# The values' projection: hi and lo weights side by side in one product of 512 columns, the halves added by GpSimd

## The chip, the core and the metric

The kernel runs on one core of a Trainium2 chip. The metric is the device time of one execution in microseconds. The core has TensorE (PE; its weight loads are shown as PEld), VectorE (DVE), ScalarE (ACT), GpSimd (POOL) and SyncE (SP). SP issues nearly all DMAs here; it, like every engine, works through its instructions in program order, and each waits on semaphores for what it reads or overwrites.

## The reference

A decoder block over 1024 tokens of width 1024, in float32. What matters here:

```
h = rms_norm(x, g_pre_mix)
z = h @ w_in
q, k, v, glu_in, z_ga, z_gc = split(z)
y_attn = dilated_attention_mixer(q, k, v, rel_bias_table, w_attn_out)
y_conv = conformer_conv_mixer(glu_in, ...)
merged = sigmoid(z_ga) * y_attn + sigmoid(z_gc) * y_conv
x = x + rms_norm(merged @ w_mix_out, g_post_mix)
x = x + rms_norm(swiglu_ffn(rms_norm(x, g_pre_ffn), w_ffn_in, w_ffn_out), g_post_ffn)
```

The values `v` are `h` (1024 x 1024) times 1536 columns of `w_in`: three dilated groups of eight heads of 64 columns.

## The kernel before

Every matrix product keeps float32 accuracy by splitting both operands in two parts, `hi` (rounded to fp32r) and `lo` (the rest), and adding three products: hi·hi, hi·lo and lo·hi. A split is a copy on ScalarE (hi) and a subtraction on VectorE or GpSimd (lo = x - hi).

Tiles of 128 x 1024 come from a pool of 42 slots (`slot()`, names `b`), of 3 (`ring()`, `d`) and, at half the width, of 11 (`half()`, `c`). Whoever takes a slot again waits for its last reader. PSUM has eight banks; in the stage at hand two of them have the tag `g` and serve the values' projection, two each `s`, `t` and `o` serve the attention.

The order on every engine is the order of the program text, written out by hand. `tick()` counts steps of work on TensorE: it runs what `later(n, step)` planned for that tick, takes one pending weight split from `pieces` at every fourth tick (`PIECE = 4`) and advances the background generators. `beat()` paces one generator more finely: every call adds `RATE` (0.42 in this stage) to a credit, and each whole credit advances `fine`, here `attention()`, by one step.

The program in order: the gate and GLU projections with the convolution beside them, the query and key projections (each stored to HBM), then the stage of the values, then the convolution's output projection, the attention's output projection, the mixing product, and the feed-forward part (its weight products are `unit`, L305 to L309, and `prod`, L321 to L323).

The stage of the values is six calls of `v(g, hg, now, then)`, one for each group and half of its heads. A call computes 8 tiles of 128 tokens by 256 columns, over KT = 8 slices of the contraction. Before the change, two tiles share a bank of 512 columns, in two accumulation groups; each slice is three products of 256 columns (L948: hi tokens with hi weights; L950: hi tokens with lo weights; L952: lo tokens with hi weights), each followed by a `beat()`, and every second slice by a `tick()`. After two tiles ScalarE copies the bank to a tile of the ring (L960 for group 0, L963 for the others); after four tiles, five ticks later, the tile goes to HBM (L933, L935). `timed()` loads the next call's weights at the fourth tick (L177) and queues their splits from the sixteenth tick on (`part()`, L188 and L189): each call has two weight tiles of 128 x 1024 (4 slices each), and each tile is split in two pieces of 512 columns.

Beside it run, in this order:

- `conv_norm()`, the normalisation of the convolution's output (L1265 to L1296): sums on TensorE, squares, `rstd()` (L402 to L411, transposes L417), then for each of eight blocks a product on VectorE (L1292), a SiLU on ScalarE (L1295) and a store (L1296).
- `attention()`, which starts in earnest when that is done (`normed` at 9). It goes over pairs of heads ("stacks"), eight query blocks each. `stack_load()` loads the queries' and keys' parts (L870 to L877) and the bias (L479); `double()` copies them to the other half of the partitions on GpSimd, two copies for each of two heads and each half of the tokens (L886, L887); `values()` loads the stored values (L898 to L903) and `value_parts()` splits them (ScalarE L917, GpSimd L918 and L922). The first stack is doubled directly before its first scores; a later one during query blocks 6 and 7 of the stack before.
- Per query block: scores on TensorE (`att_s`, L1049), bias and minimum on VectorE (L1052), one step later the exponential on ScalarE (`att_e`, L1062), four steps later transposes on TensorE (`att_t`, L1087) and a split (L1094, L1095), five steps later the products with the values (`att_p`, L1122).

`wsplit`, the engine that takes the subtraction of second weight pieces, is GpSimd while the queries and keys are projected and VectorE in the stage of the values.

Of the kernel before, what the change touches and what calls it, by code (L numbers as in the profile page):

```python
# [58 lines left out]
def f(ap):  # L59
    return ap.bitcast(F32)  # L60


class Build:
# [115 lines left out]

    def part(self, i, c):  # L180
        nc = self.nc
        n = self.jobs[i][1]
        s = slice(c * n // 2, (c + 1) * n // 2)
        if c == 0:
            self.hl[i] = (self.slot(F32R), self.slot(F32R))
        hi, lo = self.hl[i]
        r = self.raw[i]
        nc.scalar.copy(hi[:, s], r[:, s])  # L188
        (nc.vector if c == 0 else self.wsplit).tensor_tensor(lo[:, s], r[:, s], f(hi[:, s]), op=OP.subtract)  # L189
        if c == 1:  # L190
            del self.raw[i]

# [732 lines left out]
    def v(self, g, hg, now, then):  # L925

        nc = self.nc
        W = self.timed(now, then, 4, 16)

        def out(i, x):  # L930
            for e in range(2):
                if g == 0:
                    nc.sync.dma_start(self.d_v[g, 2 * hg + e][:, (i - 2) * 128:(i + 2) * 128], x[:, e * H:(e + 1) * H])  # L933
                    continue
                nc.sync.dma_start(self.d_v[g, 2 * hg + e].rearrange("(t p) c -> p t c", p=128)[:, i - 2:i + 2],  # L935
                                  x.rearrange("p (t e c) -> p t e c", t=4, e=2)[:, :, e])
            self.vn += i == 6

        for i in range(0, 8, 2):
            ps = self.bank()  # L940
            for e in range(2):
                t = slice((i + e) * 128, (i + e + 1) * 128)
                o = ps[:, e * 256:(e + 1) * 256]
                for kt in range(KT):
                    hi, lo = W[kt // 4]
                    s = slice((kt % 4) * 256, (kt % 4 + 1) * 256)
                    a, b = self.hH[kt][:, t], self.hL[kt][:, t]
                    nc.tensor.matmul(o, a, hi[:, s], start=kt == 0, stop=False)  # L948
                    self.beat()
                    nc.tensor.matmul(o, a, lo[:, s], start=False, stop=False)  # L950
                    self.beat()
                    nc.tensor.matmul(o, b, hi[:, s], start=False, stop=kt == KT - 1)  # L952
                    self.beat()
                    if kt % 2:
                        self.tick()
            if i % 4 == 0:
                x = self.ring()

            if g == 0:
                nc.scalar.copy(x.rearrange("p (e t c) -> p t e c", e=2, t=4)[:, i % 4:i % 4 + 2],  # L960
                               ps.rearrange("p (t e c) -> p t e c", t=2, e=2))
            else:
                nc.scalar.copy(x[:, (i % 4) * 256:(i % 4) * 256 + H], ps)  # L963
            if i % 4:
                self.later(5, lambda i=i, x=x: out(i, x))
                x = None

# [433 lines left out]
def build(ctx, tc, aps):  # L1401
# [18 lines left out]
    ga = [pair(NGA + n, NGA + n + 1) for n in range(0, 8, 2)]  # L1420
    gc = [pair(NGC + n, NGC + n + 1) for n in range(0, 8 - LATE - EARLY, 2)]
    qkj = {(g, hp): pair(NK + 4 * g + hp, NQ + 4 * g + hp) for g in range(3) for hp in range(4)}
    vj = {(g, hg): (job(aps["w_v"][2 * g + hg, 0]), job(aps["w_v"][2 * g + hg, 1], kind="second"))
          for hg in range(2) for g in range(3)}
    late = [job(w_in[NGC + n]) for n in range(8 - LATE - EARLY, 8 - EARLY)]
    co = [job(aps["w_co"][n]) for n in range(8)]
# [107 lines left out]
    B.OT, B.merges = {}, []  # L1534
    cn = B.bg(B.conv_norm())
    att = B.attention()
    vs = list(vj.values()) + [late[:1] or co[:1]]
    for i, (g, hg) in enumerate(vj):
        B.v(g, hg, vs[i], vs[i + 1])
        if i == 0:  # L1540
            next(att)
            B.fine = att
        elif i == 4:
            assert cn not in B.gens
            cs = []
            B.later(16, lambda: cs.append(B.bg(B.conv_split())))
    B.RATE = RU

    B.PIECE = 3
# [485 lines left out]
```

## Time and profile before

| | us |
|---|---|
| median of 3 runs | 1713.83 (1711.94 to 1715.37) |
| the profiled execution | 1713.53 |
| its span in the profile | 1711.4 |
| stage of the values in it (first to last product of L948 to L952) | 550.8 to 793.8 |
| first scores of the attention | 615.1 |

How to read the rows shown below. In the page's first part an engine has its busy time, the share of the span and the number of instructions. A timeline row has start and duration in us, engine, line, operation, what is written and read (partitions x elements), the count, and in brackets the idle time before it with what ended it. A group's row ends in busy time and mean ns of one, and after the bar the idle time of the engine before its instructions. A row that begins with a stretch A:B has its length, then the busy time (and count) of PE, PEld, DVE, ACT and POOL, or of PE and PEld alone where only one line was asked for, then the granted TensorE clock, the busy share of the DMA engines and GB/s. A row of waits has who waited, for whom, total us, times, and the longest. In the chain of waits each row has start, duration and what the chain went through; "issue" is time for which the profile names no cause.

### The profile page before, as it was taken

To read this page: it belongs to the slowest core of one execution; us is meant where nothing else is said; L and a number is where in the kernel's file an instruction comes from. 1 tells how busy PE (TensorE), PEld (TensorE's weight loads), DVE (VectorE), ACT (ScalarE), POOL (GpSimd) and SP (SyncE) were. 2 spreads that over 40 slices of the span, in tenths; PEclk is the share of its full clock that TensorE was granted. 3 is DMA by queue.
4 is the path that set the end of the run, shared out by engine and by line. 5 is a ranking of instruction groups with operands and counts; after the bars stand their busy time and mean duration, and the time that the engine had idled before them with its cause. 6 is when DMAs were issued, how large, how long until landed. Compare 5 with 4: busy or idle time off the path is not lost.

```text
span 1711.4 us, 24544 instructions
## 1 busy us (share of the span) xinstructions
PE 1692.6 (99%) x8758; PEld 1437.4 (84%) x8758; DVE 1251.5 (73%) x2214; ACT 790.1 (46%) x1550; POOL 470.0 (27%) x373
## 2 busy tenths in 40 slices
PE   8999999999999999999999999999999999999998
PEld 6788888888888999999778888888888888888886
DVE  6789988888998667677885855775566556677686
ACT  6344344434444576676722436633333333354463
POOL 0017777887886124444300210000000000000000
PEclk9999999999999999999999999999999999999999
DMA  4352434455568887878998722123222322494334
GB/s 166 103 185 87 148 124 130 155 193 174 173 167 206 249 261 208 234 204 229 295 274 281 266 79 99 68 95 127 93 92 103 119 93 92 148 374 144 103 130 154
DMA packets 162422, 283.43 MB, mean 166 GB/s; under 512 B 47249, under 2 KB 78796, under 8 KB 162300
## 3 DMA queue, kind: packets, MB, share of 16 engines
q1 hardware_dynamic: 161644, 281.23, 51.9%
q8 instruction: 69, 1.13, 0.3%
q0 software_dynamic: 368, 0.37, 0.1%
q14 instruction: 53, 0.43, 0.1%
q10 hardware_dynamic: 288, 0.27, 0.0%
HBM read 191.10 MB, written 95.42 MB: 167 GB/s over the span
## 4 chain that ended last, share of the span: by engine, by line
PE 91%; DMA 3%; ACT 2%; DVE 2%; issue 1%; POOL 1%; SPq 0%; DVEq 0%; ACTq 0%; POOLq 0%
PE p L321 16%; PE p L322 16%; PE p L323 16%; PE p L1919 12%; PE p L1648 5%; PE p L305 4%; PE p L307 4%; PE p L309 4%; PE p L1122 3%; PE p L948 2%; PE p L950 2%; PE p L952 2%; PE p L1049 2%; PE p L1087 2%; DMA b<-xT 1%
## 5 line engine op out<-in xcount | busy, mean ns | idle before, releaser
L321 PE MATMUL p<-b,b 128*128 128x512 f32 x1204 | 468.6, 389 | 0.3 <-ACT c L340 0.3
L322 PE MATMUL p<-b,b 128*128 128x512 f32 x1204 | 468.4, 389 | 0.0
L323 PE MATMUL p<-b,b 128*128 128x512 f32 x1204 | 468.4, 389 | 0.0
L321 PEld LDWEIGHTS p<-b,b 128*128 128x128 f32 x1204 | 226.0, 188 | 47.9 <-ACT c L340 0.7
L323 PEld LDWEIGHTS p<-b,b 128*128 128x128 f32 x1204 | 226.0, 188 | 46.9
L322 PEld LDWEIGHTS p<-b,b 128*128 128x128 f32 x1204 | 226.0, 188 | 46.9
L1919 PE MATMUL p<-b,b 128*128 128x512 f32 x924 | 209.6, 389 | 0.0
L1919 PEld LDWEIGHTS p<-b,b 128*128 128x128 f32 x924 | 173.4, 188 | 36.0
L686 DVE SCALAR_TENSOR_TENSOR p<-b,par,p 128x511 f32<-128x511 f32 (+14 forms) x232 | 163.6, 739 | 0.0
L305 PE MATMUL p<-b,b 128*128 128x512 f32 x368 | 146.7, 399 | 1.4 <-ACT b L1242 1.2
L307 PE MATMUL p<-b,b 128*128 128x512 f32 x368 | 145.5, 395 | 0.0
L309 PE MATMUL p<-b,b 128*128 128x512 f32 x368 | 145.5, 395 | 0.0
L195 ACT CAST b<-d 128x1024 fp32r<-128x1024 f32 x86 | 90.4, 1051 | 105.1 <-POOL d L216 55.1
L196 POOL TENSOR_TENSOR b<-d,b 128x1024 fp32r<-128x1024 f32 x44 | 106.9, 2429 | 79.7 <-ACT b L195 72.4
L196 DVE TENSOR_TENSOR b<-d,b 128x1024 fp32r<-128x1024 f32 x42 | 51.3, 1222 | 101.0 <-ACT b L195 101.0
L948 PE MATMUL p<-b,b 128*128 128x256 f32 x384 | 112.8, 294 | 0.0
L952 PE MATMUL p<-b,b 128*128 128x256 f32 x384 | 112.2, 292 | 0.0
L950 PE MATMUL p<-b,b 128*128 128x256 f32 x384 | 112.2, 292 | 0.0
L1243 DVE TENSOR_TENSOR b<-b,b 128x512 fp32r<-128x512 f32 x133 | 91.6, 693 | 22.2 <-ACT b L1242 20.1
L1242 ACT CAST b<-b 128x512 fp32r<-128x512 f32 x133 | 82.1, 619 | 46.8 <-PE p L1919 18.0
L1648 PE MATMUL p<-b,b 128*128 128x512 f32 x384 | 89.4, 391 | 0.0
L1062 ACT ACTIVATE c<-c,stat 128x128 f32<-128x128 f32 (+1 forms) x192 | 85.0, 446 | 5.6 <-DVE stat L1052 5.3
(233 smaller groups left out, 2995.5 us busy)
## 6 DMA issues: line engine op xcount, KB each, us to landing
b<-w_in SPq DMA_DIRECT2D x30, 512.0 KB, 5.0
dk<-c SPq DMA_DIRECT2D x48, 256.0 KB, 2.9
dq<-c SPq DMA_DIRECT2D x48, 256.0 KB, 3.7
b<-dq SPq DMA_DIRECT2D x48, 256.0 KB, 5.1
b<-dk SPq DMA_DIRECT2D x48, 256.0 KB, 7.5
b<-w_fi SPq DMA_DIRECT2D x24, 512.0 KB, 5.0
d<-w_in SPq DMA_DIRECT2D x23, 512.0 KB, 4.3
dqS<-c SPq DMA_DIRECT2D x44, 256.0 KB, 2.0
```

The lines of the kernel that those rows point to most:

```text
L196: self.wsplit.tensor_tensor(lo, x, f(hi), op=OP.subtract)
L305: nc.tensor.matmul(ps, hi[:, s], a, start=kt == 0, stop=False)
L307: nc.tensor.matmul(ps, hi[:, s], b, start=False, stop=False)
L309: nc.tensor.matmul(ps, lo[:, s], a, start=False, stop=kt == nk - 1)
L321: nc.tensor.matmul(ps, hi[:, s], a, start=first and kt == 0, stop=False, skip_group_check=True)
L322: nc.tensor.matmul(ps, hi[:, s], b, start=False, stop=False, skip_group_check=True)
L323: nc.tensor.matmul(ps, lo[:, s], a, start=False, stop=kt == 3, skip_group_check=True)
L686: nc.vector.scalar_tensor_tensor(A[i][:, j:], src[i][:, :H - j], w[i], A[i][:, j:], op0=OP.mult, op1=OP.add)
L948: nc.tensor.matmul(o, a, hi[:, s], start=kt == 0, stop=False)
L950: nc.tensor.matmul(o, a, lo[:, s], start=False, stop=False)
L1648: nc.tensor.matmul(banks[tt][nh], st, wt[:, nh * H:(nh + 1) * H], start=bool(kt == 0 and a), stop=bool(kt == KT - 1 and b))
L1919: nc.tensor.matmul(acc[t], x, y, start=first and e == 0, stop=last and e == 2, skip_group_check=True)
```

## The change

The weights of the values are laid out in other order: for each slice of the contraction, 256 columns of hi and 256 of lo stand side by side. A slice is then two products: the hi tokens with all 512 columns into the whole bank (hi·hi in its left half, hi·lo in its right half), and the lo tokens with the 256 hi columns, accumulated on the right half. `beat()` is called three times per slice as before, twice after the first product and once after the second.

A bank now belongs to one tile of tokens. ScalarE copies it to one half of a new tile `vsum` (one slot, held for the whole stage); after every second tile GpSimd adds the left and right halves of both into the ring's tile. The stores wait for that add. The splits of these weights write to the new layout (`value_weights`), with the subtraction always on VectorE, and each weight tile is given up in the last token tile, slice pair by slice pair. `job(..., kind="values")` marks the first weight tile so that `part()` sends it there.

```diff
     def part(self, i, c):
         nc = self.nc
+        if self.jobs[i][2] in ("values", "second"):
+            return self.value_weights(i, c)
...
+    def value_weights(self, i, c):
+
+        x = self.slot(F32R)
+        self.hl.setdefault(i, []).append(x)
+        r = self.raw[i][:, c * H:(c + 1) * H].rearrange("p (k n) -> p k n", k=2)
+        d = x.rearrange("p (k e n) -> p k e n", k=2, e=2)
+        self.nc.scalar.copy(d[:, :, 0], r)
+        self.nc.vector.tensor_tensor(d[:, :, 1], r, f(d[:, :, 0]), op=OP.subtract)
+        if c == 1:
+            del self.raw[i]
...
     def v(self, g, hg, now, then):
...
-        W = self.timed(now, then, 4, 16)
+        W = [x for w in self.timed(now, then, 4, 16) for x in w]
...
-        for i in range(0, 8, 2):
-            ps = self.bank()
-            for e in range(2):
-                t = slice((i + e) * 128, (i + e + 1) * 128)
-                o = ps[:, e * 256:(e + 1) * 256]
-                for kt in range(KT):
-                    hi, lo = W[kt // 4]
-                    s = slice((kt % 4) * 256, (kt % 4 + 1) * 256)
-                    a, b = self.hH[kt][:, t], self.hL[kt][:, t]
-                    nc.tensor.matmul(o, a, hi[:, s], start=kt == 0, stop=False)
-                    self.beat()
-                    nc.tensor.matmul(o, a, lo[:, s], start=False, stop=False)
-                    self.beat()
-                    nc.tensor.matmul(o, b, hi[:, s], start=False, stop=kt == KT - 1)
-                    self.beat()
-                    if kt % 2:
-                        self.tick()
-            if i % 4 == 0:
+        for i in range(8):
+
+            ps = self.bank()
+            t = slice(i * 128, (i + 1) * 128)
+            for kt in range(KT):
+                w = W[kt // 2][:, kt % 2 * H:(kt % 2 + 1) * H]
+                a, b = self.hH[kt][:, t], self.hL[kt][:, t]
+                nc.tensor.matmul(ps, a, w, start=kt == 0, stop=kt == KT - 1, skip_group_check=True)
+                self.beat()
+                self.beat()
+                nc.tensor.matmul(ps[:, 256:], b, w[:, :256], start=False, stop=kt == KT - 1, skip_group_check=True)
+                self.beat()
+                w = None
+                if kt % 2:
+                    if i == 7:
+                        W[kt // 2] = None
+                    self.tick()
+            nc.scalar.copy(self.vsum[:, i % 2 * H:(i % 2 + 1) * H], ps)
+            if i % 2 == 0:
+                continue
+            if i % 4 == 1:
                 x = self.ring()
 
+            y = self.vsum.rearrange("p (t k n) -> p k t n", t=2, k=2)
+            d = x[:, i % 4 // 2 * H:(i % 4 // 2 + 1) * H].rearrange("p (t n) -> p t n", t=2)
             if g == 0:
-                nc.scalar.copy(x.rearrange("p (e t c) -> p t e c", e=2, t=4)[:, i % 4:i % 4 + 2],
-                               ps.rearrange("p (t e c) -> p t e c", t=2, e=2))
-            else:
-                nc.scalar.copy(x[:, (i % 4) * 256:(i % 4) * 256 + H], ps)
-            if i % 4:
+                y = y.rearrange("p k t (e c) -> p k e t c", e=2)
+                d = x.rearrange("p (e t c) -> p e t c", e=2, t=4)[:, :, i % 4 - 1:i % 4 + 1]
+            nc.gpsimd.tensor_tensor(d, y[:, 0], y[:, 1], op=OP.add)
+            if i % 4 == 3:
                 self.later(5, lambda i=i, x=x: out(i, x))
                 x = None
...
     att = B.attention()
+
+    B.vsum = B.slot()
     vs = list(vj.values()) + [late[:1] or co[:1]]
...
+    B.vsum = None
     B.RATE = RU
```

The stores' slices and the count `vn` are shifted by one tile accordingly, from `i - 2 : i + 2` at i = 6 to `i - 3 : i + 1` at i = 7.

More of the change, by code (lines that the diff above doesn't have):

```diff
@@ L932, in out @@
                 if g == 0:
-                    nc.sync.dma_start(self.d_v[g, 2 * hg + e][:, (i - 2) * 128:(i + 2) * 128], x[:, e * H:(e + 1) * H])
+                    nc.sync.dma_start(self.d_v[g, 2 * hg + e][:, (i - 3) * 128:(i + 1) * 128], x[:, e * H:(e + 1) * H])
                     continue
-                nc.sync.dma_start(self.d_v[g, 2 * hg + e].rearrange("(t p) c -> p t c", p=128)[:, i - 2:i + 2],
+                nc.sync.dma_start(self.d_v[g, 2 * hg + e].rearrange("(t p) c -> p t c", p=128)[:, i - 3:i + 1],
@@ L936, in out @@
                                   x.rearrange("p (t e c) -> p t e c", t=4, e=2)[:, :, e])
[L937 to L939 removed]
+            self.vn += i == 7
+        for i in range(8):
             ps = self.bank()
[L941 to L956 removed]
+            t = slice(i * 128, (i + 1) * 128)
[16 more added lines that the diff above has]
+            if i % 4 == 1:
@@ L1422, in build @@
     qkj = {(g, hp): pair(NK + 4 * g + hp, NQ + 4 * g + hp) for g in range(3) for hp in range(4)}
-    vj = {(g, hg): (job(aps["w_v"][2 * g + hg, 0]), job(aps["w_v"][2 * g + hg, 1], kind="second"))
+    vj = {(g, hg): (job(aps["w_v"][2 * g + hg, 0], kind="values"), job(aps["w_v"][2 * g + hg, 1], kind="second"))
           for hg in range(2) for g in range(3)}
```

## The prediction

> **What bounds the kernel now.** I read the page first, then the stage that the diff touches, then what every other engine and queue does around it. The page:
>
> ```profile
> span 1711.4 us, 24544 instructions
> PE 1692.6 (99%) x8758; PEld 1437.4 (84%) x8758; DVE 1251.5 (73%) x2214; ACT 790.1 (46%) x1550; POOL 470.0 (27%) x373
> PEclk9999999999999999999999999999999999999999
> ```
>
> TensorE sets the end nearly everywhere, at full granted clock. The profiled execution took 1713.53 us, 2.1 us more than its span; the median shown is 1713.83 (1711.94 to 1715.37), so the two agree and I add my sum to 1713.53.
>
> The stage of the values is found by its first product (L948), once for each of 6 calls x 8 token tiles x 8 slices of the contraction = 384:
>
> ```profile
> 550.70:612.70 62.00, 45.83 (x160) 30.65 (x161) 1.00 0.87 264
> 612.70:794.10 181.40, 66.96 (x224) 42.43 (x224) 1.00 0.78 222
> ```
>
> 160 = 2 x 64 + 32, so at 612.70 two calls and half of the third are done, almost alone on TensorE: 62 us for 160 slices. The other 224 slices take 181 us, because from 615 on the attention's products stand between them. What the other engines do meanwhile, in the order PE, PEld, DVE, ACT, POOL:
>
> ```profile
> 552.00:590.00 38.00, 38.00 (x310) 37.04 (x309) 23.87 (x27) 17.14 (x25) 7.74 (x8) 1.00 0.93 282
> 600.00:614.00 14.00, 14.00 (x119) 14.00 (x118) 5.41 (x6) 7.57 (x9) 0.00 (x0) 1.00 1.01 309
> 630.00:670.00 40.00, 40.00 (x371) 40.00 (x371) 28.71 (x91) 26.25 (x82) 18.04 (x26) 1.00 0.74 207
> ```
>
> In the mixed part ScalarE is busy two thirds, VectorE 72%, GpSimd 45%: room for more work, if it isn't late. Before 615 GpSimd is all but idle and the DMA engines are full (1.01). Both matter below. The row of the order in which TensorE meets the attention:
>
> ```profile
> 601.07 0.28 PE L952 MATMUL p<-b,b 128*128 128x256 f32 x1
> ...
> 612.71 0.28 PE L948 MATMUL p<-b,b 128*128 128x256 f32 x1
> ...
> 614.99 0.28 PE L950 MATMUL p<-b,b 128*128 128x256 f32 x1
> 615.11 0.56 PE L1049 MATMUL p<-b,b 128*128 128x128 f32 x4
> 615.50 0.33 PE L952 MATMUL p<-b,b 128*128 128x256 f32 x1
> ...
> 620.39 0.74 PE L1049 MATMUL p<-b,b 128*128 128x256 f32 x4 [0.63 <-DVE stat L1052]
> ...
> 622.45 0.83 PE L1122 MATMUL p<-c,b 128*66 128x256 f32 x3 [0.40 <-POOL b L918]
> ```
>
> The displayed 0.28 us of a product is latency. What it costs TensorE is the distance of starts: 612.71 to 614.99 is 19 distances, 0.120 us each. The attention's first products (L1049) come at 615.11, after 20 products of the fifth tile (i = 4) of the third call. The only idle TensorE time in the stage is the 0.63 and 0.40 us while the attention's pipeline fills.
>
> **The change, part by part.** *The products.* For the price of 512 columns with a fresh stationary operand, the feed-forward part:
>
> ```profile
> 1299.83 0.39 PE L322 MATMUL p<-b,b 128*128 128x512 f32 x1
> ...
> 1303.91 0.39 PE L322 MATMUL p<-b,b 128*128 128x512 f32 x1
> ```
>
> This is 18 distances in 4.08 us, 0.2267 us each. A slice costs 3 x 0.1200 = 0.3600 now and 0.2267 + 0.1200 = 0.3467 then: 13.3 ns saved. The columns streamed stay 768; what goes is one product's fixed share. Over 384 slices: -5.1 us. The displayed means (294 for 256 columns, 389 for 512) would promise 384 x 0.2 = 76 us; they are latencies, and I don't use them. The attention's steps are paced by three calls of beat() per slice as before, so their number and the weight loads exposed after them stay.
> The Trainium skill, "TensorE: Matmul & The Clock Gate", section "Back-to-back issue gap", gives a warm product N/2.4 + 2.5 ns. By it three products of 256 cost 327 and the pair 325 ns, and the gain would be 0.9 us, the sum 4.2 us higher; the measured distances of 120 and 227 have about 13 ns of fixed share, so I keep 5.1.
>
> *Copies, adds and splits.* Prices from the stage's groups:
>
> ```profile
> L963 ACT COPY d<-p 128x512 f32<-128x512 f32 x15 | 8.7, 583 | 6.5 <-PE p L952 6.3
> L960 ACT COPY d<-p 128x512 f32<-128x512 f32 x8 | 4.7, 588 | 7.8 <-PE p L952 7.7
> L918 POOL TENSOR_TENSOR b<-b,b 128x512 fp32r<-128x512 f32 x18 | 23.1, 1282 | 100.2 <-ACT b L917 85.1 <-PE p L1122 7.9 <-ACT c L1062 7.2
> L189 DVE TENSOR_TENSOR b<-b,b 128x512 fp32r<-128x512 f32 x22 | 15.6, 711 | 15.1 <-ACT b L188 14.6 <-POOL b L886 0.2
> ```
>
> ScalarE empties a bank per tile: 48 copies for 24, 24 x 0.585 = 14 us more in 243. GpSimd gets 24 adds of 1.28 us, 31 us. The weight splits keep count and size; the second half of the first jobs moves from GpSimd to VectorE, where one takes 0.71 us; 0, and 0.71 us if the first slices wait for it. None of this is on TensorE's path by its sum. Its order is.
>
> *What the add is put in front of.* GpSimd now, over the whole early stage, and ScalarE around 614:
>
> ```profile
> 549.19 2.39 POOL L708 TENSOR_TENSOR b<-b,b 128x1024 f32<-128x1024 f32 x1
> 574.03 1.43 POOL L886 CAST b<-b 64x512 fp32r<-64x512 f32 x1 [22.46 <-DMA b<-dq]
> ...
> 583.07 0.61 POOL L887 CAST b<-b 64x512 fp32r<-64x512 f32 x1
> 619.58 1.28 POOL L918 TENSOR_TENSOR b<-b,b 128x512 fp32r<-128x512 f32 x1 [35.89 <-ACT b L917]
> ...
> 622.75 0.61 POOL L886 CAST b<-b 64x512 fp32r<-64x512 f32 x1
> ...
> 627.79 0.61 POOL L887 CAST b<-b 64x512 fp32r<-64x512 f32 x1
> ```
>
> ```profile
> 593.04 1.08 ACT L1288 COPY b<-p 128x512 f32<-128x512 f32 x2 [2.93 <-PE p L417]
> ...
> 603.88 0.56 ACT L963 COPY d<-p 128x512 f32<-128x512 f32 x1
> ...
> 607.75 0.56 ACT L963 COPY d<-p 128x512 f32<-128x512 f32 x1
> 614.13 0.62 ACT L188 CAST b<-b 128x512 fp32r<-128x512 f32 x1 [5.82 <-issue]
> 614.65 0.58 ACT L963 COPY d<-p 128x512 f32<-128x512 f32 x1
> 615.25 1.28 ACT L1062 ACT_TABLE_LOAD   x1
> ```
>
> ```profile
> 606.91 1.42 DMA b<-w_v
> 608.32 5.81 issue
> ```
>
> The eight copies of double() (L886, L887) for the first pair of heads run at 574 to 584, over 30 us before TensorE needs them, because GpSimd has nothing ahead of them but L708. In the program they stand directly before the first L1049, in tile 4 of the third call. The change queues ten adds ahead of them; the last (i = 3 of that call) waits for ScalarE's copy of tile 3, and that copy stands behind L188, the first split of the next call's weights, issued at the sixteenth tick (the end of tile 3). L188 waits until 614.13; the chain has a load of w_v before it, and the DMA engines are full, so I read it as that load's landing.
>
> So: L188 at 614.13, copy at 614.65 to 615.23, add of 1.28 us to 616.5, then copies at a distance of 0.72 us: (627.79 - 622.75) / 7. Both heads' first halves need four, 2.9 us: 619.4. Then L1049's last two products, 0.2 us: TensorE is past its first step at 619.6, where it is at 615.50 now: +4.1. The 167 slices before that point had saved 2.2 us; that is swallowed by the wait, as are bank waits earlier on. (Two banks now hold one tile each, 2.8 us of work. Today's lag from 601.07 to the copy at 603.88 and its 0.56 us, 3.4 us, would then hold TensorE about 0.6 us, and is paid in full if the wait at 613 isn't there.) Bounds for the landing: it comes 1.3 us earlier, as TensorE reaches the transposes (L417) that ScalarE's chain starts from after some 96 faster slices, or not at all. I take -0.4, since full queues keep their own pace. Then 217 slices more: -2.9.
>
> Two further terms. The 1.03 us of idle time in the filling pipeline goes or stays: the table load has time before the first scores now, but one more copy of 0.58 is in ScalarE's queue; between -1.0 and +0.6, I take 0. In the mixed part 14 more copies and 13 adds stand in the queues before the attention's work; if each held TensorE for a copy's 0.585 us that is 8.2, if none 0. Nearest is 0, since ScalarE has a third of its time free and GpSimd half, and a tile lasts 181 / 28 = 6.5 us: only an add behind a whole run of eight doubles (0.6 + 5.7 + 1.3 us after the tile) comes late for the next even tile, by 1.1 us; I take +0.7.
>
> The slot for vsum takes one of 42 from the loads. SP does wait for slots:
>
> ```profile
> SPq L870 <- PE p L952: 6.7, 1, 6.7
> ```
>
> That load is the first heads' stacks, needed 30 us later; one more such wait costs nothing here, and up to 6.7 us where a load is late already. The output stores wait for the add instead of the copy, 1.3 us, and stand five ticks behind: 0.
>
> Sum: +4.1 - 0.4 - 2.9 + 0 + 0.7 = +1.5, so 1715.0 us. The likeliest outcome is that the gain pays for the late start of the attention.
>
> TensorE would then stand idle for some 4 us, up from 1.
>
> ```profile
> 0.00:5.00 5.00, 0.00 (x0) 0.00 (x0) 0.54 (x4) 1.86 (x3) 2.17 (x12) 1.00 0.58 173
> ```
>
> The granted clock is 1.00 in every stretch, and also in these 5 us without a product, so no row shows a loss after an idle time. The Trainium skill, same page, section "What's actually happening", has the clock go to half after an idle window of 3.4 us and return after as much work: by it about 1.7 us more, 1716.7.
>
> **The rivals.** *Faster: the wait isn't there.* If the load lands 4 us earlier, the copy of tile 3 starts at 610.9 with the tile's end, the add ends at 612.8, four copies at 615.7, TensorE goes on at 615.9, +0.4, and with -2.9 and the +0.7 the end is 1711.7. If GpSimd's copies are out of the way altogether, all 5.1 us arrive: 1708.4. For it: the unnamed 5.81 us may be another thing than the load. Against it: the order on GpSimd, which is fixed by the program.
>
> *Slower: the eight copies at their price of 574.* There the first took 1.43 us, not 0.61, with the DMA engines as full as at 614. Four at 1.5 us instead of 0.72 are 3.1 us more: 1718.1. It decides from about 1.3 us each. Against it: at 622.75 they take 0.61.
>
> *Slower: ScalarE and GpSimd late in the mixed part.* The single vsum makes the copy of an even tile wait for the add before, and everything on ScalarE behind it: the upper bound of 8.2 instead of 0.7 gives 1722.5, half of it 1718.4. For it: GpSimd works in runs of eight copies, 5.7 us, and the attention's exponentials and casts share ScalarE's queue. Against: a tile's 6.5 us.
>
> *No gain from the wide product.* Then +2.9 is not given back: 1717.9 or more. The measured 0.2267 us speaks against it. And behind the stage the DMA engines are full:
>
> ```profile
> 834.00:844.00 10.00, 8.73 (x64) 7.12 (x63) 9.47 (x37) 6.63 (x24) 1.39 (x2) 1.00 1.04 397
> ```
>
> TensorE misses 1.3 us there now, so a shift of a few us may be stretched or absorbed by about as much; this widens every case.
>
> **How the numbers follow.** Late start paid by the gain: 0.45, with 1711.5 to 1718 as its own range. Faster: 0.22 (1708.4 to 1711.7). Copies at the dear price: 0.15. Late queues in the mixed part: 0.14. No gain: 0.04. Within 0.2% (3.4 us, what a measurement of this kernel can tell from no change) of 1713.83 is 1710.4 to 1717.3. The main case lies there but for 0.05 at its top; the faster case reaches over with 0.04; of the slower ones 0.03 falls short of it. Faster 0.18, same 0.47, slower 0.35. The range from 1708.5 to 1721 leaves the ends of the outer cases out.
>
> **What would show it.** Right: the first L886 after 615 and after an add; an idle TensorE of 3 to 5 us before the first L1049, ended by GpSimd; distances of 0.227 and 0.120 in the values' products; 48 copies and 24 adds near 0.58 and 1.28 us. Wrong: the doubles still at 574, no idle time there, or a new idle time at a bank in every tile.

## The result, and the profile after

| | us, median | beside before | ratio, 95% interval |
|---|---|---|---|
| changed kernel, first measurement, 16 runs | 1718.79 (1715.03 to 1722.06) | 1713.78 | 1.0033 [1.0024, 1.0041] |
| changed kernel, second measurement, 11 runs | 1716.35 (1714.41 to 1718.21) | 1713.21 | 1.0019 [1.0010, 1.0027] |

The change makes the kernel slower, by 0.2 to 0.3%: 5.0 us by the first measurement's medians, 3.1 by the second's. The forecast was 1715.0 with a range from 1708.5 to 1721; both medians lie in the range, above the forecast, and the first also lies above 1718, where the prediction's likeliest case ended; by the bound of 0.2% the first is slower and the second at its edge. The profiled execution took 1717.66 us, its span 1715.9, 4.5 more than the span of before.

The first rows of the changed kernel's page:

```profile
span 1715.9 us, 23845 instructions
PE 1694.7 (99%) x8374; PEld 1414.1 (82%) x8374; DVE 1259.9 (73%) x2216; ACT 802.2 (47%) x1574; POOL 496.4 (29%) x395
```

TensorE has 384 instructions fewer and is busy 2.1 us longer. The number of products alone therefore says little of the time; the place to look is where TensorE stands. Stretches of the stage in the changed kernel (length, then PE, PEld, DVE, ACT, POOL, granted clock, DMA share, GB/s):

```profile
600.00:614.00 14.00, 12.55 (x71) 10.46 (x70) 8.00 (x7) 10.14 (x12) 2.89 (x2) 1.00 0.94 276
616.00:619.30 3.30, 1.20 (x6) 0.68 (x4) 0.69 (x1) 2.04 (x3) 2.34 (x3) 1.00 1.09 385
619.30:626.10 6.80, 6.20 (x23) 5.54 (x24) 3.11 (x16) 3.56 (x12) 3.81 (x7) 0.51 1.06 345
630.00:670.00 40.00, 40.00 (x327) 36.25 (x326) 29.38 (x90) 28.75 (x87) 20.66 (x27) 1.00 0.65 178
```

There are two holes, one in 600 to 614 (before: full) and one in 616 to 619.3, and behind the second the granted clock is 0.51 for 6.8 us. In 630 to 670 TensorE is full again, though ScalarE and GpSimd have more to do than before. The same in the changed kernel's timeline of TensorE (L959 is the product of 512 columns, L962 the one of 256; in brackets the idle time and what ended it):

```profile
548.40 0.39 PE L336 MATMUL p<-b,b 128*128 128x512 f32 x1
548.98 0.50 PE L334 MATMUL p<-b,b 128*128 128x512 f32 x1 [0.19 <-DVE c L853]
...
560.59 0.40 PE L959 MATMUL p<-b,b 128*128 128x512 f32 x1
560.83 0.28 PE L962 MATMUL p<-b,b 128*128 128x256 f32 x1
...
562.71 0.40 PE L959 MATMUL p<-b,b 128*128 128x512 f32 x1
...
601.14 0.28 PE L962 MATMUL p<-b,b 128*128 128x256 f32 x1
602.84 0.50 PE L959 MATMUL p<-b,b 128*128 128x512 f32 x1 [1.42 <-ACT b L969]
...
616.48 0.39 PE L959 MATMUL p<-b,b 128*128 128x512 f32 x1
618.84 0.33 PE L1066 MATMUL p<-b,b 128*128 128x128 f32 x1 [1.97 <-POOL b L899]
619.51 0.47 PE L1066 MATMUL p<-b,b 128*128 128x128 f32 x1 [0.34 <-POOL b L900]
620.17 0.48 PE L1066 MATMUL p<-b,b 128*128 128x128 f32 x1 [0.20 <-POOL b L899]
620.84 0.47 PE L1066 MATMUL p<-b,b 128*128 128x128 f32 x1 [0.19 <-POOL b L900]
621.12 0.52 PE L962 MATMUL p<-b,b 128*128 128x256 f32 x1
```

A slice is one of each: six slices from 560.59 to 562.71 are 0.353 us each, 0.236 and 0.117. The scores (now L1066) start at 618.84, and each of their four products waits for one of GpSimd's copies; TensorE is past this step at 621.12, where before it was at 615.50. Of the two queues that set this, the changed kernel's timeline of ScalarE:

```profile
615.65 0.62 ACT L201 CAST b<-b 128x512 fp32r<-128x512 f32 x1 [3.18 <-DMA b<-w_v]
616.18 0.58 ACT L969 COPY b<-p 128x512 f32<-128x512 f32 x1
```

And its timeline of GpSimd:

```profile
616.84 1.28 POOL L980 TENSOR_TENSOR d<-b 128x512 f32<-128x512 f32 x1 [4.99 <-ACT b L969]
618.18 0.60 POOL L899 CAST b<-b 64x512 fp32r<-64x512 f32 x1
618.84 0.61 POOL L900 CAST b<-b 64x512 fp32r<-64x512 f32 x1
```

Read in order of time, this is the chain of the prediction link by link: the load of w_v lands and releases the split (L201) at 615.65, the bank's copy follows at 616.18, the add at 616.84, and the first of the eight doubles (L899), at 574.03 before, only at 618.18. The groups of the copies and adds between 550 and 800 us have about the prices that were used (the adds before 600 take up to 1.78 us, hence the mean of 1379 ns):

```profile
L980 POOL TENSOR_TENSOR d<-b 128x512 f32<-128x512 f32 x23 | 31.7, 1379 | 79.7 <-ACT b L969 60.2 <-DMA b<-dq 6.6 <-PE p L1139 6.4
L969 ACT COPY b<-p 128x512 f32<-128x512 f32 x48 | 28.0, 583 | 18.3 <-PE p L962 16.6 <-POOL d L980 1.5
```

For comparing kernels I use five points of TensorE's timeline, in us: the first product of the values (A), the first product of the values after the attention's first scores (B), the second pair's first scores (C), the last product that begins a slice of the values (D) and the end of the span (E).

| | A | B | C | D | E | A to B | B to C | C to D | D to E |
|---|---|---|---|---|---|---|---|---|---|
| before | 550.77 | 615.50 | 629.37 | 793.29 | 1711.4 | 64.73 | 13.87 | 163.92 | 918.1 |
| changed | 551.83 | 621.12 | 635.93 | 799.09 | 1715.9 | 69.29 | 14.81 | 163.16 | 916.8 |
| changed, second profile | 551.51 | 620.38 | 634.43 | 797.60 | 1714.8 | 68.87 | 14.05 | 163.17 | 917.2 |

The loss is in A to B, +4.6 and +4.1 us. C to D gives back 0.8. A itself lies between 550.7 and 552.3 in the profiles of all the kernels below, so that its 1.1 is mostly spread between executions.

### The profile page after: what moved, and what is told of

Same layout as the page of the kernel before. It is cut to its first block, busy times and chain, and to the rows that moved or that the text cites. A ratio compares the mean times of both kernels' runs of the same rounds, so it can differ in the third digit from the quotient of the medians.

```text
span 1715.9 us, 23845 instructions
## 1 busy us (share of the span) xinstructions
PE 1694.7 (99%) x8374; PEld 1414.1 (82%) x8374; DVE 1259.9 (73%) x2216; ACT 802.2 (47%) x1574; POOL 496.4 (29%) x395
## 4 chain that ended last, share of the span: by engine, by line
PE 93%; DMA 2%; DVE 2%; ACT 1%; issue 1%; POOL 1%; SPq 0%; DVEq 0%; ACTq 0%; POOLq 0%
PE p L334 15%; PE p L335 15%; PE p L336 15%; PE p L1939 12%; PE p L1668 5%; PE p L318 5%; PE p L320 5%; PE p L322 5%; PE p L959 5%; PE p L1139 3%; PE p L962 2%; PE p L1066 2%; PE p L569 2%; PE p L1104 2%; DMA dact<-b 1%
## 5 line engine op out<-in xcount | busy, mean ns | idle before, releaser
L334 PE MATMUL p<-b,b 128*128 128x512 f32 x1204 | 468.8, 389 | 0.5 <-ACT c L353 0.3
L335 PE MATMUL p<-b,b 128*128 128x512 f32 x1204 | 468.4, 389 | 0.0
L336 PE MATMUL p<-b,b 128*128 128x512 f32 x1204 | 468.4, 389 | 0.0
L1939 PE MATMUL p<-b,b 128*128 128x512 f32 x924 | 209.6, 389 | 0.0
L959 PE MATMUL p<-b,b 128*128 128x512 f32 x384 | 150.2, 410 | 1.4 <-ACT b L969 1.4
L318 PE MATMUL p<-b,b 128*128 128x512 f32 x368 | 146.6, 398 | 1.3 <-ACT b L1259 1.2
L320 PE MATMUL p<-b,b 128*128 128x512 f32 x368 | 145.6, 396 | 0.0
L322 PE MATMUL p<-b,b 128*128 128x512 f32 x368 | 145.5, 395 | 0.0
L962 PE MATMUL p<-b,b 128*128 128x256 f32 x384 | 116.0, 302 | 0.0
L1668 PE MATMUL p<-b,b 128*128 128x512 f32 x384 | 89.4, 391 | 0.0
L208 ACT CAST b<-b 128x1024 fp32r<-128x1024 f32 x47 | 49.5, 1052 | 82.0 <-POOL b L236 37.2
```

The source lines that it names most:

```text
L318: nc.tensor.matmul(ps, hi[:, s], a, start=kt == 0, stop=False)
L320: nc.tensor.matmul(ps, hi[:, s], b, start=False, stop=False)
L322: nc.tensor.matmul(ps, lo[:, s], a, start=False, stop=kt == nk - 1)
L334: nc.tensor.matmul(ps, hi[:, s], a, start=first and kt == 0, stop=False, skip_group_check=True)
L335: nc.tensor.matmul(ps, hi[:, s], b, start=False, stop=False, skip_group_check=True)
L336: nc.tensor.matmul(ps, lo[:, s], a, start=False, stop=kt == 3, skip_group_check=True)
```

## The experiments

The theory: the late start of the attention is the whole loss, and it comes from the order on GpSimd alone. The rivals: the longer way from the bank costs throughout the stage; the wide product is worth nothing; the clock's drop is the loss. Each diff is against the changed kernel unless it says otherwise.

**The doubles ahead of the adds.** The add stays on GpSimd; the eight copies are put into its queue as soon as the convolution's normalisation has begun.

```diff
+        doubled = False
...
                     while self.normed < 9 or x is None:
+                        if not doubled and self.normed:
+                            doubled = True
+                            self.double(nxt, 0)
+                            self.double(nxt, 1)
...
-                    if cur is None:
-                        self.double(nxt, 0)
-                        self.double(nxt, 1)
```

> The first stack's eight copies of double() are put on GpSimd as soon as the first block of the normalisation is done, some 15 us before the first scores; all else as in the changed kernel. Theory (the loss is the order on GpSimd, plus the half clock that follows the idle time): no wait before the first scores, which come at about 616.7 instead of 618.84, TensorE past the first step at 617.1 instead of 621.1, granted clock 1.00 throughout; time 4 to 6 us under the changed kernel, about 1713 to 1715, no different from before. Rival (the loss is in banks, copies and the mixed part): time stays above 1717.

Measured: 1714.04, ratio 1.0008 [0.9997, 1.0019]. GpSimd's timeline of this kernel has the doubles at 592 to 601, between two adds; they cost up to 1.6 us each there:

```profile
592.03 0.96 POOL L899 CAST b<-b 64x512 fp32r<-64x512 f32 x1
...
595.06 1.63 POOL L899 CAST b<-b 64x512 fp32r<-64x512 f32 x1
...
599.33 1.49 POOL L900 CAST b<-b 64x512 fp32r<-64x512 f32 x1
...
616.51 1.31 POOL L980 TENSOR_TENSOR d<-b 128x512 f32<-128x512 f32 x1 [4.20 <-ACT b L969]
```

The timeline of TensorE in the same kernel has no wait between the wide product, the scores (L1069 here) and the next product:

```profile
617.22 0.40 PE L959 MATMUL p<-b,b 128*128 128x512 f32 x1
617.46 0.56 PE L1069 MATMUL p<-b,b 128*128 128x128 f32 x4
617.85 0.33 PE L962 MATMUL p<-b,b 128*128 128x256 f32 x1
```

B is at 617.85, 3.3 us earlier than in the changed kernel's first profile and 2.5 than in its second; A to B is 65.53, 3.8 and 3.3 us less. B to C is 14.05, C to D 163.19. The late add, its wait for the load and every later copy and add are still there. What costs is that the doubles stood behind them. The interval reaches to no loss, and not to a gain of more than 0.03%: something else holds the promised gain back. A part of it is a hole at a bank, in the same timeline of TensorE:

```profile
601.63 0.28 PE L962 MATMUL p<-b,b 128*128 128x256 f32 x1
603.69 0.50 PE L959 MATMUL p<-b,b 128*128 128x512 f32 x1 [1.77 <-ACT b L969]
```

ScalarE's copy of that bank waits 0.92 us for an add that now stands behind the doubles and ends at 603.02.

**The add on VectorE.** GpSimd has its old order back, and VectorE the adds.

```diff
-            nc.gpsimd.tensor_tensor(d, y[:, 0], y[:, 1], op=OP.add)
+            nc.vector.tensor_tensor(d, y[:, 0], y[:, 1], op=OP.add)
```

> The halves are added by VectorE instead of GpSimd; all else as in the changed kernel. Theory (order on GpSimd): GpSimd's first eight copies go back to 574 to 584, no wait for GpSimd before the first scores, clock 1.00; time about 1713 to 1715. The add takes 0.7 instead of 1.3 us. Rival (VectorE, which now waits for ScalarE's copy with everything behind it, is late for the attention): new idle time of TensorE that VectorE ends, time above 1717.

Measured: 1713.56, ratio 0.9998 [0.9988, 1.0009]. An add takes VectorE 0.76 us (mean of 24). By its timeline of GpSimd the doubles run at 575 to 588, about as before the change:

```profile
574.75 6.98 POOL L899 CAST b<-b 64x512 fp32r<-64x512 f32 x1 [28.59 <-DMA b<-dq]
...
587.05 0.61 POOL L900 CAST b<-b 64x512 fp32r<-64x512 f32 x1
```

TensorE comes past the scores at 616.78. The late start is gone, the loss is gone, and no gain has come. This kernel's timeline of TensorE shows part of the reason:

```profile
600.51 0.28 PE L962 MATMUL p<-b,b 128*128 128x256 f32 x1
601.68 0.50 PE L959 MATMUL p<-b,b 128*128 128x512 f32 x1 [0.90 <-ACT b L969]
...
607.58 0.28 PE L962 MATMUL p<-b,b 128*128 128x256 f32 x1
608.42 0.50 PE L959 MATMUL p<-b,b 128*128 128x512 f32 x1 [0.56 <-ACT b L969]
```

From the last product of a tile to the first of the next are 1.17 and 0.84 us here, where 0.12 is the distance without a wait: 1.05 and 0.72 us lost because ScalarE empties the bank late. In its queue the two copies, at 601.06 and 607.80, stand behind the convolution's SiLUs (L1312, 1.25 us each) and, the first, a weight split. These are the bank waits that the prediction put at 0.6 us and hid under the wait at 616. With that wait gone they show: A to B is 65.58, not less than the 64.73 of before.

**The old products in the new data flow.** Three products of 256 columns again, with the new weight layout, the copy of every tile and the add on GpSimd kept.

```diff
-                nc.tensor.matmul(ps, a, w, start=kt == 0, stop=kt == KT - 1, skip_group_check=True)
+                nc.tensor.matmul(ps[:, :256], a, w[:, :256], start=kt == 0, stop=kt == KT - 1, skip_group_check=True)
                 self.beat()
+                nc.tensor.matmul(ps[:, 256:], a, w[:, 256:], start=False, stop=kt == KT - 1, skip_group_check=True)
                 self.beat()
```

> The changed kernel with three products of 256 columns per slice again (hi.hi in the left half, hi.lo and lo.hi in the right), bank per tile, copy and GpSimd add kept. Theory: same wait before the first scores and same half clock. The wide product and its partner took 0.353 us per slice in the changed kernel against 0.360 before, so what the 217 slices after the wait give back is 1.5 us: about 1720.3. If the pair were worth the 13.3 ns of the prediction: 1721.7. If the wide product is worth nothing beside the attention: 1718.8.

Measured: 1718.53, ratio 1.0027 [1.0018, 1.0036], between the changed kernel's two. Taking the wide product away costs nothing that the time shows. In the trace C to D is 163.98 us, as before the change (163.92), and 163.16 to 163.20 in the seven profiles of kernels that have the wide product beside each narrow one and copy every bank to `vsum`: 0.8 us for the 203 slices there, 4 ns a slice.

**Warm or idle.** Nine products whose result nobody reads fill TensorE's wait before the first scores.

```diff
                         self.double(nxt, 1)
+                        ps = self.bank("o")
+                        for i in range(9):
+                            self.nc.tensor.matmul(ps, self.hH[0][:, :128], self.hH[0][:, :H], start=i == 0, stop=i == 8)
+                        ps = None
```

> Nine products of 512 columns into an unused bank (their result is never read) are issued before the first scores, where TensorE idles for 2.1 us in the changed kernel; the waits stay as they are. Theory (the idle time brings the clock to half until 626, and that costs by itself): the clock stays at 1.00, and the second stack of heads begins 1.5 to 2.5 us earlier relative to the first scores; time about 1716.5 to 1717.3. Rival (the clock's record costs nothing, the waits alone do): time as in the changed kernel, 1718.8, or up to 0.5 us more.

Measured: 1717.4, ratio 1.0023 [1.0013, 1.0032]. In this kernel's stretches the granted clock stays at 1.00 where it was 0.51:

```profile
616.00:619.30 3.30, 2.91 (x15) 2.10 (x13) 0.08 (x1) 1.14 (x1) 3.06 (x4) 1.00 1.13 353
619.30:626.10 6.80, 6.28 (x41) 5.23 (x41) 4.04 (x21) 5.31 (x17) 4.67 (x8) 1.00 1.05 366
```

41 products go through in those 6.8 us, 23 in the changed kernel's profile. But the ratio's interval overlaps with the changed kernel's, [1.0024, 1.0041], so both were run once more.

**Both once more, side by side.** The changed kernel as it is, and the one with nine products.

> The changed kernel as it is, beside the one with the nine products before the first scores, on the same chip. Theory: ratio to before 1.0025 to 1.004, half clock for 3.4 or 6.8 us after the wait.

> The nine products of 512 columns in TensorE's idle time before the first scores, again. Theory (half clock costs by itself): clock at 1.00 there, 1 to 2 us under the changed kernel of this call. Rival (the half clock is hidden behind the attention's filling pipeline): within 0.5 us of it.

Measured: 1716.35, 1.0019 [1.0010, 1.0027], and 1716.6, 1.0027 [1.0016, 1.0037]. The changed kernel comes out below the 1.0025 to 1.004 that was expected, and the nine products bring no gain. This time the stretches of the changed kernel have much the same wait at 616 and full clock behind it:

```profile
616.00:619.30 3.30, 1.42 (x7) 0.76 (x5) 0.36 (x1) 1.40 (x2) 2.92 (x4) 1.00 1.11 366
619.30:626.10 6.80, 6.03 (x40) 5.10 (x41) 4.04 (x21) 5.05 (x17) 4.61 (x8) 1.00 1.06 360
```

So the drop comes in some executions and not in others; the kernel with the old products has one too, half as long, in this stretch:

```profile
622.20:625.60 3.40, 3.40 (x18) 3.40 (x17) 2.80 (x13) 3.38 (x12) 1.58 (x4) 0.50 1.06 373
```

From the traces its price is small: B to C is 14.81 with 6.8 us of half clock and 14.05 without, 0.8 us; the old products with 3.4 us of it have 13.96. The runs that were not profiled have their mean granted clock on record. In the first measurement of the changed kernel 13 of 16 runs stand at 0.996 or 0.997, in the second 4 of 11, and beside it 3 of 25 runs of before; none of the 21 runs with the nine products does. So a lower clock is common in the changed kernel, and the nine products take it away, yet they gain nothing that the times show.

The rival that the clock is the whole loss falls: the second profile has A to B of 68.87 at full clock. The runs at 0.999, where that profile stands, agree. Their spans are 1713.5 and 1713.7 us for the changed kernel (two runs in each measurement) and 1710.3 for before (14 runs beside the second): 3 us are lost there without it. A lower clock goes with longer runs, 1718.3 us in the first measurement's eight runs at 0.996, but also with longer runs of before, 1714.4 in the three at 0.997; what the drop behind the wait adds to the first measurement's median stays open.

**Why is the wide product worth so little?** Four kernels take the products apart, on top of the add on VectorE. The first groups products of one width: two wide ones, then two narrow ones.

```diff
...
-                self.beat()
-                nc.tensor.matmul(ps[:, 256:], b, w[:, :256], start=False, stop=kt == KT - 1, skip_group_check=True)
                 self.beat()
                 w = None
                 if kt % 2:
+                    for k in (kt - 1, kt):
+                        w = W[k // 2][:, k % 2 * H:k % 2 * H + 256]
+                        nc.tensor.matmul(ps[:, 256:], self.hL[k][:, t], w, start=False, stop=k == KT - 1, skip_group_check=True)
+                        self.beat()
...
```

> On the kernel with the add on VectorE: for every two slices first the two wide products, then the two of 256 columns; sums and places as before. If the wide product's 0.236 us (0.2267 in the feed-forward part) comes from changing between 512 and 256 columns, half the changes go: a pair of slices falls from 0.707 to about 0.693 us in the part without attention, and the time by 1 to 2.5 us. If it comes from the operands or the bank, the distances stay 0.236 and 0.117 in sum, and the time stays within 1 us of the kernel with the add on VectorE.

Measured: 1713.11, ratio 1.0000 [0.9988, 1.0013]. In its timeline of TensorE (L958 wide, L965 narrow), two slices reach from one pair of wide products to the next, and nine such distances from the first row to the last:

```profile
559.06 0.63 PE L958 MATMUL p<-b,b 128*128 128x512 f32 x2
559.52 0.40 PE L965 MATMUL p<-b,b 128*128 128x256 f32 x2
...
565.33 0.63 PE L958 MATMUL p<-b,b 128*128 128x512 f32 x2
```

Two slices take 6.27 / 9 = 0.697 us, against 2 x 0.3533 = 0.707 alternating. That is 5 ns a slice better, near the 0.693 that was expected if the changes of width cost. It doesn't show in the time: 1 to 2.5 us less were expected, and the ratios to before are 1.0000 and, with the add on VectorE alone, 0.9998. Beside the attention little of it is left: from C to the last product of the values are 163.52 us, and 163.59 with the add on VectorE alone. The second puts the narrow product on the left half of the bank, so that it doesn't follow on the half that the wide one has just written.

```diff
-                nc.tensor.matmul(ps[:, 256:], b, w[:, :256], start=False, stop=kt == KT - 1, skip_group_check=True)
+                nc.tensor.matmul(ps[:, :256], b, w[:, :256], start=False, stop=kt == KT - 1, skip_group_check=True)
```

> On the kernel with the add on VectorE: the product of the lo tokens goes to the left half of the bank (added to hi.hi) instead of the right half, which the wide product has written last. If the 9 ns come from accumulating on columns just written, the wide product falls to 0.227 us and a slice to 0.347, and the time by up to 2.6 us; if not, 0.236 and 0.117 stay and so does the time.

Measured: 1713.67, ratio 1.0008 [0.9997, 1.0018]; the distances stay at 0.236 and 0.117 (medians of the part before 600). The half of the bank isn't it. The third makes both products 512 columns wide.

```diff
-                nc.tensor.matmul(ps[:, 256:], b, w[:, :256], start=False, stop=kt == KT - 1, skip_group_check=True)
+                nc.tensor.matmul(ps, b, w, start=False, stop=kt == KT - 1, skip_group_check=True)
```

> On the kernel with the add on VectorE: the lo tokens also meet all 512 columns, so lo.lo is computed too and every product of the stage has 512 columns. If products of 512 columns are dear with these operands, they stay at 0.233 to 0.236 us; if a neighbour of 256 columns makes them so, they fall to 0.227, as in the feed-forward part. The time itself rises by 384 x 0.107 = 41 us or more.

Measured: 1759.24, one run. Its timeline of TensorE, eight distances from the first to the last row:

```profile
559.97 0.39 PE L959 MATMUL p<-b,b 128*128 128x512 f32 x1
...
561.79 0.39 PE L959 MATMUL p<-b,b 128*128 128x512 f32 x1
```

1.82 / 8 = 0.2275 us, within the rows' 0.01 us the feed-forward part's price, with the operands, the layout and the bank of the changed kernel. So none of these makes the wide product dear; its neighbours do. A slice that alternates has two changes of width and takes 0.353 us, two by two it has one and takes 0.348, and the uniform streams add up to 0.347. By what mechanism a change of width costs, no run here shows. The fourth is the grouped kernel with the second pieces' subtraction given back to GpSimd for the first jobs (`self.wsplit`):

```diff
-        self.nc.vector.tensor_tensor(d[:, :, 1], r, f(d[:, :, 0]), op=OP.subtract)
+        (self.nc.vector if c == 0 else self.wsplit).tensor_tensor(d[:, :, 1], r, f(d[:, :, 0]), op=OP.subtract)
```

> The add on VectorE, products grouped by width, and the second weight pieces subtracted as before the change: the three pieces that each cost least so far. The 0.35 us of idle time before the first values product goes. Time 0.3 to 0.6 us under the same kernel without the last piece: ratio to before 0.9990 to 1.0000, so hardly to be told from before.

Measured: 1711.66, ratio 0.9996 [0.9985, 1.0007]. In its timeline TensorE no longer waits for L853 ahead of the stage, as expected. This is the best of the variants, and its interval holds 1: no gain is shown.

**Without the longer way.** No `vsum`, no GpSimd: ScalarE copies 256 columns of the bank to the ring, VectorE adds the other 256 from the bank; the subtraction goes as in the last one.

```diff
-            nc.scalar.copy(self.vsum[:, i % 2 * H:(i % 2 + 1) * H], ps)
...
-            nc.gpsimd.tensor_tensor(d, y[:, 0], y[:, 1], op=OP.add)
+            nc.scalar.copy(d, y[:, 0])
+            nc.vector.tensor_tensor(d, y[:, 1], d, op=OP.add)
```

> No tile vsum and no add on GpSimd: ScalarE copies the left 256 columns of the bank to the ring's tile, VectorE adds the right 256 from the bank. The second piece of each weight tile is subtracted by the engine that did it before the change (GpSimd for the first call). Theory (late queues before the first scores, nothing in the mixed part): first scores when TensorE gets there; its idle time for the banks near 600, 1.1 and 0.7 us with the add on VectorE, shrinks, since a copy of 256 columns is shorter; the 0.35 us before the first values product goes. Time 1711 to 1713, ratio to before 0.999 to 1.000. Rival (VectorE in the way of the bank's release as ScalarE was): as the kernel with the add on VectorE, 1.000, or above.

Measured: 1714.68, ratio 1.0014 [1.0005, 1.0022], slower than before. Now the bank waits for VectorE, whose timeline has the convolution's long products (L1290, L1296) in front of the add (L978):

```profile
574.16 1.22 DVE L1290 TENSOR_TENSOR b<-b,b 128x1024 f32<-128x1024 f32 x1
575.30 1.22 DVE L1296 TENSOR_TENSOR b<-b,b 128x1024 f32<-128x1024 f32 x1
576.43 0.42 DVE L978 TENSOR_TENSOR d<-p,d 128x256 f32<-128x256 f32 x1
```

TensorE, in the same kernel's timeline, meanwhile:

```profile
575.12 0.28 PE L962 MATMUL p<-b,b 128*128 128x256 f32 x1
576.91 0.49 PE L959 MATMUL p<-b,b 128*128 128x512 f32 x1 [1.51 <-DVE d L978]
```

That is a hole of 1.67 us beyond the product's 0.12. In this profile TensorE also stands twice at 754, behind the attention's work on ScalarE and VectorE, and C to D is 164.26. The same edit together with the grouping of the products:

> The kernel with the right half added from the bank, with the products of two slices grouped by width. If the change of width costs: 1 to 2.5 us under the same kernel ungrouped, about 1709 to 1711, the first that is faster than before. If not: the same time as that one.

Measured: 1713.69, ratio 1.0008 [1.0000, 1.0017]. That is 1.0 us under the ungrouped one, with intervals that overlap, and not faster than before. A shorter way isn't a faster one where the engine that it ends on is busy.

## Why the prediction was right, and where it was not

The chain that makes the loss came link by link as forecast. The forecast time was too low mostly because the gain that was to pay for it was put too large; the range holds both medians because the rivals had made it wide.

*The late start* (+4.1): right, mechanism and size. From the landing's release (L201 at 615.65) to TensorE past its first step (621.12) are 5.47 us, 5.37 in the second profile; the prediction's own chain from 614.13 to 619.6 is 5.47. That it agrees to the hundredth is luck. The first two experiments show the cause: with the doubles ahead of the adds, or the adds on another engine, the step waits for nothing. Of the signs that the prediction named, the doubles behind an add, the 48 copies and 24 adds and the idle time ended by GpSimd came, though TensorE's idle time is 2.7 us in four pieces and not 3 to 5; the distances of 0.227 and 0.120 did not come.

*The load's landing* (-0.4): wrong in sign. L201 is released 1.52 us later than before; with A's 1.06 taken off, +0.46 stays, and +0.13 in the second profile. The issue of that load moved from 606.91 to 608.30 in the changed kernel's timeline of SP:

```profile
608.30 1.10 SPq L177 DMA_DIRECT2D b<-w_v  x2
```

TensorE's faster slices didn't bring it forward. In SP's queue it stands behind stores of the convolution, which wait for SiLUs on ScalarE; the last store ahead of it is issued at 605.75, and at 604.33 before. So the delay is there ahead of the load, in the convolution's chain; which of its links made it, no run was made to show. In A to B the sum of both terms, +3.7, measured +4.6 and +4.1.

*The gain of 13.3 ns a slice* (-5.1 in all, -2.9 behind the wait): this is the step that failed. The prediction put together 0.2267 from a stream of nothing but wide products and 0.1200 from one of nothing but narrow ones. Side by side they take 0.353, a gain of 6.7 ns alone on TensorE and, by C to D, of 4 ns beside the attention: 0.8 us behind C. Every slice before the wait is swallowed, as forecast. The rival "no gain from the wide product", at 0.04, was nearer in size than the forecast, and its 1717.9 near the time, between the two medians. By the formula of the Trainium skill, "TensorE: Matmul & The Clock Gate", section "Back-to-back issue gap", which the page gives for an isolated product, the gain would be an estimated 2.5 ns a slice; the trace differs, since the distances are 236 and 117 ns and not its 216 and 109. The prediction's "4.2 us higher" for that case counts all 384 slices, though its sum holds only the 217 behind the wait: 2.9 less 0.5 would have made it 2.4 us higher, 1717.4.

*The filling pipeline* (0): right. B to C is 14.05 without the clock's drop, 13.87 before.

*The bank waits* (0.6, hidden): larger, 1.58 us (601.14 to 602.84, less 0.12), but hidden in the changed kernel, since what ends the wait at 616 hangs on the load, the copy and the add and not on TensorE. They show where that wait is taken away.

*The subtraction on VectorE* (0 to 0.71): a part came, just ahead of the stage, by the changed kernel's timeline of VectorE:

```profile
544.46 3.49 DVE L202 TENSOR_TENSOR b<-b,b 128x512 fp32r<-128x512 f32 x2
547.87 1.05 DVE L853 TENSOR_TENSOR c<-p,c 128x512 f32<-128x512 f32 x1
```

L853 stands behind two subtractions now; before, the second was GpSimd's. The first is the long one. It takes 2.88 us, where it took 0.68 before, while GpSimd's product L721, which came forward from 549 to 543.94 with the subtraction gone from its queue, runs until 546.79 beside it. In TensorE's timeline above the product at 548.98 waits for L853: 0.58 us after the one before, 0.35 more than 0.23. The three kernels that give the second subtraction back to GpSimd don't have this wait. The spread of A hides whether it lasts.

*Late queues in the mixed part* (+0.7, at most 8.2): fell. From 630 to 799 TensorE waits for nothing, and C to D is shorter with all copies and adds in place; with the old products and the same copies and adds it is as long as before. (The adds left for that part are 14, not 13.)

*The clock* (outside the sum): the row of before couldn't decide it. Half clock came behind the wait in one of two profiles of the changed kernel and cost about 0.8 us there. The Trainium skill, same page, section "What's actually happening", has the clock drop after about 3.4 us of idle time, with a window that runs freely: the traces agree that it drops behind the wait, for 6.8 and 3.4 us, and that much the same wait doesn't always bring it; the idle time here is shorter, 2.0 us and three gaps of 0.2 to 0.3.

*The doubles at the dear price* (rival, 1718.1): fell. They take 0.61 us at 618, with the DMA engines at 1.09; the time came out near 1718 for another reason.

As a sum for the first profile: A +1.1, A to B +4.6, B to C +0.9, C to D -0.8, D to E -1.3 make +4.5 us of span; for the second +0.7, +4.1, +0.2, -0.8, -0.9 make +3.4 by the unrounded spans. The forecast of +1.5 counted on 2.9 us paid back behind the wait and on 0.4 from an earlier load; 0.8 was paid back, and the load came later. The -1.3 and -0.9 behind the stage lie within what the prediction allowed there, about 1.3 us stretched or absorbed.

## What to carry to other kernels

On an engine that works in program order, ask of every added instruction not what it costs but what stands behind it: an add of 1.3 us that hangs on a late load moved eight copies by 44 us, and the first four of them set TensorE back by 4. A distance of products measured in a uniform stream is not the price in a mixed one; look for a place where the two widths already alternate, or allow for half the gain, and keep products of one width together where that is free. And where a long wait is removed, the shorter ones that lay under it come out, here 1.8 us at the banks.

## What the runs showed of the hardware

Products of 512 columns take 0.227 us among their like and 0.236 in a stream with products of 256, which take 0.120 among theirs and 0.117 there. Half of the 13.3 ns a slice is lost by that when the widths alternate. Two by two gives back 5 ns of it, the other half of the bank nothing. And a granted clock of 0.5 can come behind an idle time of 2 us followed by four small products with gaps, in one execution and not in the next; in the one stretch where it could be compared, 14.81 us against 14.05, it cost under 1 us.
